# The head norm of the attention: mean squares on every row from one product with a block matrix

## The chip, the cores and the metric

One core of one Trainium2 chip runs the whole program. The metric is the device time in microseconds of one execution, from the first to the last instruction. The core has five engines that run side by side, each with a queue of its own: TensorE (PE in the profile; PEld is its loading of weights), VectorE (DVE), ScalarE (ACT), GpSimd (POOL) and SyncE (SP), which here issues the transfers. The kernel's products land in PSUM, in which it keeps eight tiles of 128 rows by 512 fp32 columns: four for the large products (`d`), three for everything else (`z`), one for the attention's sums (`acc`).

## The reference

One layer of a decoder with two head groups side by side, for a prompt of 2048 rows and for 8 x 8 sampled rows, with D = 1024:

```python
h = rmsnorm(x, norm_mix) * (1 + sc_m) + sh_m
proj = h @ w_in                                  # retention q,k,v,gate | stick-breaking q,k,v
ro = retention(...)                              # 4 heads of 128
so = sb_attention(qs, k_all, v_all, sb_bias, q_pos0)   # 8 heads of 64
so = so * lax.rsqrt(jnp.mean(so * so, axis=-1, keepdims=True) + EPS) \
    * sb_gn.reshape(H_SB, D_SB)[None, :, None, :]
mix = jnp.concatenate([ro, so], axis=-1) @ w_out
x = x + g_m * mix
# then adaLN, a gated MLP (D_FF 2816, causal convolution of width 3), residual, final RMSNorm
```

The change is in the line with `lax.rsqrt`: every head of the stick-breaking attention, 64 numbers for each token, is divided by the root of its mean square (plus EPS = 1e-6) and multiplied by a gain for each of its 64 features.

## The kernel before

All values are fp32. The large products split both operands into a high part of type fp32r and the rest, and take three of the four products (`mm3`, L295 to L297). A weight tile goes through `w_split` (L266): ACT casts the high part (`split`, L174), DVE subtracts to get the low part (`tt`, L159), both into `whl` tiles, of which there are six, two for each weight tile. Almost all tensor-tensor operations of DVE and POOL have line L159, almost all casts L174, so that they are told apart by their tiles.

The prompt is worked on in four blocks of 512 tokens. The work is written as generators, and `_weave` traces several of them side by side, each at a rate that lets all end together; the tile framework then sets the waits, and the order that each engine gets is the one that the timelines show. There are these stages:

- the start (modulation, the first rows), then the input projection `in_block` beside the attention of the sampled rows, `decode`, up to some 870 us;
- the rest of the input projection, the retention (`retention`, L966 to L1024, with `group_norm`, L939) and the attention of block 0, up to some 1260 us;
- output projection and MLP of blocks 0 to 2 (`out_block`, `ffn_block`), beside the attention of blocks 1 to 3, up to some 2935 us;
- the MLP of block 3.

`attention` goes through units (block, pair of heads j, head a of the pair, block of keys s) in four steps each. A step turns the attention weights of five steps ago (`turn`, L1150, with the split into `ahl`), multiplies those of six steps ago by the values into `acc` (`av`, L1162), and computes the scores of this one (`qk`, L1121): two sigmoids on ACT (L1124, L1125, tiles `aom` and `abe`), on POOL a mask for blocks on the diagonal (L1128, L1132) or a copy of one column (`acy`, L1135, L1141), on DVE a running product (L1138) and a multiplication (L159, `abe`). When both heads of a pair are done, `o2` holds 128 rows, two heads of 64 features, by 512 tokens, and `post` normalises it with `sb_norm` (L431 to L462), one part of it in each of the following steps of the attention: it is a generator, and its `yield` hands over to the step.

`sb_norm` before: ACT squares (L436); for each 128 tokens PE multiplies the squares by a matrix of two columns, `bo2`, which gives tokens on rows and the two heads as columns (L440, 8 columns); DVE copies them out (L442); POOL takes mean, EPS and the power -1/2 (`rstd_of`, L377 and L159 with `nhalf`, a constant tile of -0.5) and splits the result into a high and a low part (L448 to L450); PE turns it back (L454); ACT copies it (L456); PE spreads it over 128 rows with `sel4` (L459); DVE multiplies o, the gain and this (L461). In `decode` the same runs four times on 64 columns, one after the other.

Of the kernel before, what the change touches and what calls it, by code (L numbers as in the profile page):

```python
# [13 lines left out]
P = 128  # L14
# [25 lines left out]
def _consts():  # L40
# [45 lines left out]
    selb[:HS] = np.arange(HS)[:, None] == rh[None, :]  # L86
    bo2 = np.zeros((P, 2))
    bo2[:64, 0] = 1
    bo2[64:, 1] = 1
    sel4 = np.zeros((P, P))  # L90
    sel4[0, :64] = sel4[2, :64] = 1
    sel4[1, 64:] = sel4[3, 64:] = 1
    fold = np.zeros((P, 9))
# [5 lines left out]
    for t in range(NS):  # L99
        sels[1 + t // DS, t] = sels[10 + t // DS, t] = sels[18, t] = 1  # L100
    parts = dict(
        ident=ident, selb=selb, bo2=bo2, sel4=sel4, fold=fold, selp=selp, sels=sels,
        hm8=hm8, m8=m8, gsum=gsum, kdec=kdec, kdecs=kdecs, qdec=qdec, qdecs=qdecs, rowmask=rowmask,
# [16 lines left out]
class _Stream:  # L120
    """Traced work in steps; each step yields its share of the whole, or None while it has to wait."""

# [15 lines left out]
def _weave(streams, until=None):  # L138
    """Traces the streams side by side, each at the rate that lets all of them end together."""
    while any(s.live for s in streams) and (until is None or until.live):  # L140
        for s in sorted((s for s in streams if s.live), key=lambda s: s.got / s.total):
            if s.step():
                break
        else:
            raise RuntimeError("streams wait for each other")


def body(tc, I, O):
# [12 lines left out]
    def f(ap):  # L161
        return ap.bitcast(F32)
# [99 lines left out]
    def pz():  # L262
        return T(psz, [P, 512], F32, "z")

    # ------------------------------------------------------------ weights
    def w_split(src, a, b, eng=dve):  # L266
# [32 lines left out]
    def tok_mm(ps, x, w, start, stop):  # L299
        """Rows of tokens x (hi, lo) times w; a short tile has hi and lo side by side, their rows to be added."""  # L300
        if isinstance(x, tuple):
            mm3(ps, x, w, start, stop)
        else:
            pe.matmul(ps, x, w[0], start=start, stop=False)  # L304
            pe.matmul(ps, x, w[1], start=False, stop=stop)  # L305
# [40 lines left out]
    def by_tile(tiles, k0, n):  # L346
        """The products of two rows of weights with the tiles; those of the last two tile after tile."""
        order = [(k, tile) for k in range(k0, k0 + 2) for tile in tiles]
        return sorted(order, key=lambda kt: kt[1]) if k0 == n - 2 else order

    def dense_pair(wts, acts, t, features=False):
        """Two tiles of outputs, the first half of the tokens (or features) of both before the second."""
        outs = [fm_banks(t) for _ in wts]
        for h in range(2):
            for wt, out in zip(wts, outs):
                if features:
                    for ps, c0, c1 in out:
                        fm_chunk(wt, acts, ps[:, : c1 - c0], c0, c1, range(h * 4, h * 4 + 4))
                elif t == 512:
                    fm_chunk(wt, acts, out[0][0][:, h * 256 : h * 256 + 256], h * 256, h * 256 + 256)  # L360
                else:
                    ps, c0, c1 = out[h]
                    fm_chunk(wt, acts, ps[:, : c1 - c0], c0, c1)
        return outs
# [7 lines left out]

    # ------------------------------------------------------------ norms
    def rstd_of(ss, n, scale, p=P):
# [21 lines left out]
    def half_features(x, o, n, kh, A, B, acts, hpool):  # L396
        """Half kh of the columns of normalised rows, scaled and shifted, into columns o.. as hi and lo."""
        ks = slice(kh * 4, kh * 4 + 4)
# [32 lines left out]
    def sb_norm(o, n, pl, gain, tag):  # L431
        """o: [P, n], two heads of 64 rows; returns o / rms of its head * gain. Yields between its steps."""
        w = min(P, n)
        nt = n // w
        sq = T(pl, [P, n], F32, "sbsq")
        act.activation(sq, o, AF.Square)  # L436
        yield
        pm = pz()
        for t in range(nt):
            pe.matmul(pm[:w, 2 * t : 2 * t + 2], sq[:, t * w : (t + 1) * w], cc("bo2"), start=True, stop=True)  # L440
        ms = T(small, [P, 8], F32, "sbms")
        dve.tensor_copy(ms[:w, : 2 * nt], pm[:w, : 2 * nt])  # L442
        r = rstd_of(ms[:w, : 2 * nt], 2 * nt, 1.0 / DH, w)
        r4 = T(small, [P, 4, 4], F32, "sbr4")
        rh = T(small, [P, 8], F32R, "sbrh")
        rv = r[:w, : 2 * nt].rearrange("p (t a) -> p t a", a=2)
        rhv = rh[:w, : 2 * nt].rearrange("p (t a) -> p t a", a=2)
        pool.tensor_copy(rhv, rv)  # L448
        pool.tensor_copy(r4[:w, :nt, 0:2], f(rhv))
        tt(pool, r4[:w, :nt, 2:4], rv, f(rhv), ALU.subtract)  # L450
        yield
        pt = pz()
        for t in range(nt):
            pe.transpose(pt[:4, t * w : (t + 1) * w], r4[:w, t, :], ident[:w, :w])  # L454
        rt = T(pl, [P, n], F32R, "sbsq")[:4]
        act.copy(rt, pt[:4, :n])  # L456
        yield
        pb = pz()
        pe.matmul(pb[:, :n], sel4, rt, start=True, stop=True)  # L459
        out = T(pl, [P, n], F32, tag)  # L460
        dve.scalar_tensor_tensor(out, o, gain, pb[:, :n], ALU.mult, ALU.mult)  # L461
        return out  # L462

    # ------------------------------------------------------------ preparation
    def prep(pl, kp):
# [100 lines left out]

    # ------------------------------------------------------------ input projection
    def raw_features(hp, xT):
        """The first block's rows, normalised and transposed before the modulation is known."""
        for i, o, n in TILES + [(NT, TB, NS)]:  # L570
            x = T(hp, [P, D], F32, "hx")
            ld(x[:n], xp[o : o + n, :] if i < NT else xs)
            junk = T(hp, [P, D], F32, "hj")
            r = row_rstd(x, [junk[:, :512], junk[:, 512:]], n)
            dve.tensor_scalar(x[:n], x[:n], r[:n, 0:1], None, ALU.mult)
            for kh in range(2):
                ps = pz()
                for k in range(4):
                    pe.transpose(
                        ps[:, k * n : (k + 1) * n], x[:n, (kh * 4 + k) * P : (kh * 4 + k + 1) * P], ident[:n, :n]  # L580
                    )
                src = ps[:, : 4 * n].rearrange("p (k t) -> p k t", k=4)
                (act.copy if kh else dve.tensor_copy)(xT[:, kh * 4 : kh * 4 + 4, o : o + n], src)
            yield
# [165 lines left out]

    # ------------------------------------------------------------ decode attention
    def decode(dp):
# [184 lines left out]

    # ------------------------------------------------------------ retention
    def group_norm(ps, gg, qd, pl, n):  # L939
        """ps: [n, 512], four heads, each lacking its rows' decay qd; returns the gated norm of the whole."""  # L940
        mv = T(pl, [P, HR, 2], F32, "mv")
# [155 lines left out]

    # ------------------------------------------------------------ prompt attention
    def attention(blocks, tp):
# [102 lines left out]

    # ------------------------------------------------------------ output projection and MLP
    def out_block(g, xpools, fp, samp):
        """Output projection, residual and the MLP's normalised input; xpools() gives the pool of x2."""
        t = TB + (NS if samp else 0)
# [61 lines left out]
    def ffn_block(g, x2, fp, samp, after=None):  # L1268
        """The MLP and the final norm; `after` runs between the halves of the last down projection."""
        t = TB + (NS if samp else 0)  # L1270
# [123 lines left out]
    def conv_state(fi, fp):  # L1394
        """The last rows of two tiles of gates, as rows."""
        s = T(fp, [P, 512], F32, "hf")
# [22 lines left out]

    # ------------------------------------------------------------ the parts in their order  # L1420
    tile_pool = lambda name, bufs=1: tc.tile_pool(name=name, bufs=bufs, reuse_waits="tile")
    with tile_pool("in1", 2) as ip0:
        ip = _Bufs(ip0, dict(xt=2, rot=1, hf=3, st=2, kf=2, vst=1, ar=1, s18=1, gnm=1))
        with tile_pool("head", 2) as hp0:
# [17 lines left out]
            dve.tensor_scalar(nb, bb, -1.0, None, ALU.mult)  # L1442
            sel4 = T(cp, [4, P], F32R, "sel4")
            dve.tensor_copy(sel4, cc("sel4", 4))
            gnm.append(T(ip, [P, 512], F32, "gnm"))
# [61 lines left out]
class _Bufs:  # L1507
    """A pool whose tags have their own numbers of slots."""

# [9 lines left out]
class _Two:  # L1519
    """Two pools, the first for the tags given."""  # L1520

# [44 lines left out]
```

## Time and profile before

| | |
|---|---|
| median of 3 runs | 3483.96 us (3482.68 to 3484.57) |
| span of the profiled execution | 3483.6 us, 49595 instructions |
| the profiled execution's own time | given as its span alone; nothing is listed around it |
| PE, DVE, ACT, POOL busy | 3298.8, 2287.1, 1777.9, 1021.5 us |
| mean granted clock of PE | 0.979 |
| transfers | 527.72 MB, 151 GB/s over the span |

A row of a timeline has the start in us, the duration in us, engine, line, operation, output<-inputs and the count of instructions merged into it, and in brackets how long the engine sat idle before it and what ended that. A row of a stage has the stage's length, then busy time and count for PE, PEld, DVE, ACT and POOL, then the granted clock of PE, the busy share of the DMA engines, and GB/s. A row of a group has count, busy us, mean ns of one, and the idle time before them. A row of the waits has the total in us, the number of times and the longest.

### The profile page before, as it was taken

The page shows a single profiled execution, that of the slowest core. Times are in us where ns is not written, and L with a number is a line of the kernel's source. Part 1 is how long each engine was busy: PE and PEld are TensorE (multiplying, and loading weights), DVE is VectorE, ACT ScalarE, POOL GpSimd, SP SyncE. Part 2 cuts the span into 40 slices and gives each one's busy share as a digit, 9 for nine tenths or more (in the row PEclk, how much of TensorE's full clock was granted, in tenths as well). Part 3 has the DMA queues.
Part 4 walks back from the last instruction along what each step waited for, and adds up shares of the span by engine and source line. Part 5 has one row for each costly group of instructions (what it writes and reads, how often), then busy time and mean ns, then how long its engine had stood idle before and what let it go on. Part 6 is the DMA issues. An engine that isn't in the chain of part 4 may idle for free. (4 is left out here: it accounts for less than half of the span.)

```text
span 3483.6 us, 49595 instructions
## 1 busy us (share of the span) xinstructions
PE 3298.8 (95%) x17111; PEld 2693.4 (77%) x17111; DVE 2287.1 (66%) x3258; ACT 1777.9 (51%) x3153; POOL 1021.5 (29%) x1898
## 2 busy tenths in 40 slices
PE   7999999899999989999998999998899999899998
PEld 5887877776777768777877778777677777799997
DVE  5466666665665567777768777776877775545445
ACT  5457666554544456455556555554655553433323
POOL 3012011101433243434344333333433323221113
PEclk8999999999999989999999999999999999999999
DMA  6666776666756763443453333335333334332221
GB/s 226 229 198 193 234 230 218 221 223 211 210 178 194 246 196 103 121 121 112 121 182 118 118 118 112 106 112 181 109 118 106 112 103 136 112 107 88 83 86 65
DMA packets 406233, 527.72 MB, mean 151 GB/s; under 512 B 27830, under 2 KB 244009, under 8 KB 405982
## 3 DMA queue, kind: packets, MB, share of 16 engines
q1 hardware_dynamic: 405982, 524.55, 47.8%
q8 instruction: 136, 2.23, 0.3%
q14 instruction: 115, 0.94, 0.1%
HBM read 442.47 MB, written 81.99 MB: 151 GB/s over the span
## 5 line engine op out<-in xcount | busy, mean ns | idle before, releaser
L159 DVE TENSOR_TENSOR whl<-raw,whl 128x1024 fp32r<-128x1024 f32 x456 | 572.7, 1260 | 566.8 <-ACT whl L174 556.5
L174 ACT CAST whl<-raw 128x1024 fp32r<-128x1024 f32 x456 | 477.3, 1050 | 909.2 <-PE d L296 639.0
L295 PE MATMUL d<-act,whl 128*128 128x512 f32 (+2 forms) x2016 | 741.9, 369 | 5.5 <-ACT act L424 4.7
L297 PE MATMUL d<-act,whl 128*128 128x512 f32 (+2 forms) x2016 | 737.9, 366 | 4.6 <-DVE whl L159 4.6
L296 PE MATMUL d<-act,whl 128*128 128x512 f32 (+2 forms) x2016 | 735.7, 365 | 4.2 <-POOL act L159 2.2
L295 PEld LDWEIGHTS d<-act,whl 128*128 128x128 f32 x2016 | 385.8, 192 | 66.0 <-ACT act L424 6.7
L297 PEld LDWEIGHTS d<-act,whl 128*128 128x128 f32 x2016 | 385.4, 191 | 65.0 <-DVE whl L159 5.9
L296 PEld LDWEIGHTS d<-act,whl 128*128 128x128 f32 x2016 | 387.2, 192 | 60.9 <-POOL act L159 2.6
L295 PE MATMUL d<-whl,ff 128*128 128x512 f32 x704 | 280.9, 399 | 0.0
L296 PE MATMUL d<-whl,ff 128*128 128x512 f32 x704 | 280.0, 398 | 0.0
L297 PE MATMUL d<-whl,ff 128*128 128x512 f32 x704 | 279.9, 398 | 0.0
L295 PE MATMUL d<-whl,act 128*128 128x512 f32 x640 | 258.4, 407 | 14.0 <-DVE hf L159 10.8
L296 PE MATMUL d<-whl,act 128*128 128x512 f32 x640 | 259.0, 405 | 0.1
L297 PE MATMUL d<-whl,act 128*128 128x512 f32 x640 | 257.3, 403 | 0.0
L1138 DVE TENSOR_TENSOR_SCAN aom<-aom,acy 128x512 f32<-128x512 f32 x192 | 250.9, 1307 | 5.1 <-ACT aom L1124 4.6
L159 DVE TENSOR_TENSOR abe<-abe,aom 128x512 f32<-128x512 f32 (+2 forms) x320 | 234.3, 732 | 25.9 <-POOL abe L1128 5.1
L1162 PE MATMUL acc<-ahl,avv 128*128 128x512 f32 (+3 forms) x640 | 226.0, 413 | 17.6 <-ACT ahl L174 11.4
L1124 ACT ACTIVATE aom<-z,nb 128x512 f32<-128x512 f32 (+2 forms) x320 | 201.0, 628 | 73.4 <-PE z L1121 57.2
L1121 PE MATMUL z<-akk,aq 128*128 128x512 f32 (+3 forms) x640 | 193.4, 378 | 12.0 <-DVE scd L159 5.8
L1125 ACT ACTIVATE abe<-z,bb 128x512 f32<-128x512 f32 (+2 forms) x320 | 199.7, 624 | 0.0
L159 DVE TENSOR_TENSOR ahl<-z,ahl 128x512 fp32r<-128x512 f32 (+1 forms) x320 | 191.0, 597 | 11.4 <-ACT ahl L174 11.1
L159 POOL TENSOR_TENSOR ff<-ff,hf 128x512 f32<-128x512 f32 (+1 forms) x101 | 160.5, 1611 | 107.8 <-DVE hf L159 107.7
(289 smaller groups left out, 6219.4 us busy)
## 6 DMA issues: line engine op xcount, KB each, us to landing
raw<-in_w_in SPq DMA_DIRECT2D x56, 1024.0 KB
raw<-in_w_up_gate SPq DMA_DIRECT2D x44, 1024.0 KB
raw<-in_w_up_val SPq DMA_DIRECT2D x44, 1024.0 KB
akk<-k SPq DMA_DIRECT2D x160, 256.0 KB
page<-in_cache_k_pages SPq DMA_DIRECT2D x128, 256.0 KB
page<-in_cache_v_pages SPq DMA_DIRECT2D x128, 256.0 KB
raw<-in_w_down SPq DMA_DIRECT2D x32, 1024.0 KB
raw<-in_w_ada SPq DMA_DIRECT2D x24, 1024.0 KB
```

What stands on the lines that cost most here:

```text
L159: eng.tensor_tensor(o, a, b, op)
L174: act.copy(hi, src)
L295: pe.matmul(ps, sh, mh, start=start, stop=False)
L296: pe.matmul(ps, sh, ml, start=False, stop=False)
L297: pe.matmul(ps, sl, mh, start=False, stop=stop)
L1121: pe.matmul(z[:, :n], qs[g, h][:, i * P : (i + 1) * P], kk[:, c, :n], start=c == 0, stop=c == 1)
L1124: act.activation(om[:, :n], z[:, :n], AF.Sigmoid, bias=nb[:, h : h + 1], scale=-SCALE)
L1125: act.activation(be[:, :n], z[:, :n], AF.Sigmoid, bias=bb[:, h : h + 1], scale=SCALE)
L1138: dve.tensor_tensor_scan(rv, rv, rv, init, ALU.mult, ALU.bypass)
L1162: pe.matmul(accs[0][:, cs], kv[u][1][:, kt, :], m[:, cs], start=(s == g and kt == 0 and c == 0), stop=(s == 0 and kt == NT - 1 and c == 1),)
```

## The change

The mean squares of both heads come out of one product: `bo` is a 128x128 matrix with 1/64 in two blocks of 64x64 on its diagonal, so that `bo` times the squares puts the mean square of a head on each of its 64 rows, for all 512 tokens. DVE adds EPS on the way out of PSUM; POOL takes the power -1/2 of all 128x512 values in place; DVE multiplies o, the gain and the result, also in place. One tile `m` holds squares, mean squares and result one after the other. The column sums, the turn, the split and the spreading go, and with them `bo2` and `sel4`. There is an empty step between the power and the last multiplication. Both operands of the new product are plain fp32.

```diff
-    bo2 = np.zeros((P, 2))
-    bo2[:64, 0] = 1
-    bo2[64:, 1] = 1
-    sel4 = np.zeros((P, P))
-    sel4[0, :64] = sel4[2, :64] = 1
-    sel4[1, 64:] = sel4[3, 64:] = 1
+    bo = np.kron(np.eye(2), np.ones((DH, DH))) / DH
...
     def sb_norm(o, n, pl, gain, tag):
-        w = min(P, n)
-        nt = n // w
-        sq = T(pl, [P, n], F32, "sbsq")
-        act.activation(sq, o, AF.Square)
-        yield
-        pm = pz()
-        for t in range(nt):
-            pe.matmul(pm[:w, 2 * t : 2 * t + 2], sq[:, t * w : (t + 1) * w], cc("bo2"), start=True, stop=True)
-        ms = T(small, [P, 8], F32, "sbms")
-        dve.tensor_copy(ms[:w, : 2 * nt], pm[:w, : 2 * nt])
-        r = rstd_of(ms[:w, : 2 * nt], 2 * nt, 1.0 / DH, w)
-        r4 = T(small, [P, 4, 4], F32, "sbr4")
-        rh = T(small, [P, 8], F32R, "sbrh")
-        rv = r[:w, : 2 * nt].rearrange("p (t a) -> p t a", a=2)
-        rhv = rh[:w, : 2 * nt].rearrange("p (t a) -> p t a", a=2)
-        pool.tensor_copy(rhv, rv)
-        pool.tensor_copy(r4[:w, :nt, 0:2], f(rhv))
-        tt(pool, r4[:w, :nt, 2:4], rv, f(rhv), ALU.subtract)
-        yield
-        pt = pz()
-        for t in range(nt):
-            pe.transpose(pt[:4, t * w : (t + 1) * w], r4[:w, t, :], ident[:w, :w])
-        rt = T(pl, [P, n], F32R, "sbsq")[:4]
-        act.copy(rt, pt[:4, :n])
+        m = T(pl, [P, n], F32, tag)
+        act.activation(m, o, AF.Square)
         yield
         pb = pz()
-        pe.matmul(pb[:, :n], sel4, rt, start=True, stop=True)
-        out = T(pl, [P, n], F32, tag)
-        dve.scalar_tensor_tensor(out, o, gain, pb[:, :n], ALU.mult, ALU.mult)
-        return out
+        pe.matmul(pb[:, :n], cc("bo"), m, start=True, stop=True)
+        dve.tensor_scalar(m, pb[:, :n], EPS, None, ALU.add)
+        tt(pool, m, m, nhalf[:, 0:1].to_broadcast([P, n]), ALU.pow)
+        yield
+        yield
+        dve.scalar_tensor_tensor(m, o, gain, m, ALU.mult, ALU.mult)
+        return m
...
-            sel4 = T(cp, [4, P], F32R, "sel4")
-            dve.tensor_copy(sel4, cc("sel4", 4))
```

More of the change, by code (lines that the diff above doesn't have):

```diff
@@ L101, in _consts @@
     parts = dict(
-        ident=ident, selb=selb, bo2=bo2, sel4=sel4, fold=fold, selp=selp, sels=sels,
+        ident=ident, selb=selb, bo=bo, fold=fold, selp=selp, sels=sels,
         hm8=hm8, m8=m8, gsum=gsum, kdec=kdec, kdecs=kdecs, qdec=qdec, qdecs=qdecs, rowmask=rowmask,
```

## The prediction

> **What bounds the kernel now.** I read the page's first part, then the stages, then the order of time on each engine around one head norm.
>
> ```profile
> PE 3298.8 (95%) x17111; PEld 2693.4 (77%) x17111; DVE 2287.1 (66%) x3258; ACT 1777.9 (51%) x3153; POOL 1021.5 (29%) x1898
> ```
> ```profile
> 2500.00:2935.00 435.00, 430.87 (x1991) 344.89 (x1992) 327.00 (x394) 228.01 (x366) 147.31 (x249) 0.99 0.35 106
> ```
> ```profile
> 1562.13 0.39 PE L295 MATMUL d<-whl,ff 128*128 128x512 f32 x1
> ...
> 1567.49 0.40 PE L297 MATMUL d<-whl,ff 128*128 128x512 f32 x1
> ```
> ```profile
> ACT whl L174 <- PE d L296: 639.0, 226, 5.7
> ```
> TensorE (PE) is the bound: in 2500 to 2935 it is busy 430.87 of 435 us. The two matmuls are the first and last of the 24 of one split weight tile: (1567.49 - 1562.13) / 23 = 0.233 us apart, 5.6 us a tile. The wait says that ScalarE (ACT) waits for PE to give back a weight buffer (639 us in all): ACT and VectorE (DVE) run ahead of PE, by the six `whl` buffers at most. POOL, GpSimd, is 71% idle. So 1 us of PE idleness adds about 1 us to the span, and POOL costs nothing until something on PE's way waits for it.
>
> **One head norm now**, from four engines' timelines and the tile `sbsq`:
>
> ```profile
> L436 ACT ACTIVATE sbsq<-o x16: 622/632/643, 997.5 to 2913.9; 128x512 f32<-128x512 f32 x16
> ```
> ```profile
> 1540.39 0.62 ACT L436 ACTIVATE sbsq<-o 128x512 f32<-128x512 f32 x1
> ...
> 1548.01 0.56 ACT L456 CAST sbsq<-z 4x512 fp32r<-4x512 f32 x1
> ```
> ```profile
> 1541.07 1.05 PE L440 MATMUL z<-con,sbsq 128*128 128x2 f32 x8
> ...
> 1546.61 0.60 PE L454 MATMUL z<-con,sbr 128*4 128x128 f32 x4
> ...
> 1553.24 0.49 PE L459 MATMUL z<-sbsq,sel 4*128 4x512 f32 x1
> ```
> ```profile
> 1543.17 0.14 DVE L442 COPY sbms<-z 128x8 f32<-128x8 f32 x1
> ...
> 1549.28 0.67 DVE L159 TENSOR_TENSOR hf<-d,gp 128x512 f32<-128x512 f32 x1
> ...
> 1556.71 0.49 DVE L1138 TENSOR_TENSOR_SCAN aom<-aom 128x128 f32<-128x128 f32 x1 [1.25 <-POOL aom L1128]
> 1557.12 0.71 DVE L461 SCALAR_TENSOR_TENSOR sbsq<-o,vecs,z 128x512 f32<-128x512 f32 x1
> ...
> 1559.88 0.68 DVE L159 TENSOR_TENSOR ahl<-z,ahl 128x512 fp32r<-128x512 f32 x1
> ```
> ```profile
> 1544.21 1.64 POOL L159 TENSOR_TENSOR rs_b<-rs_a,nhalf 128x8 f32<-128x8 f32 x1
> ...
> 1550.02 6.38 POOL L159 TENSOR_TENSOR ff<-ff,hf 128x512 f32<-128x512 f32 x4 [3.46 <-DVE hf L159]
> ...
> 1556.39 0.29 POOL L1128 TENSOR_SCALAR_AFFINE_SELECT aom<-aom 128x128 f32<-128x128 f32 x1
> ```
> There are sixteen such norms of 128x512, one for each block and pair of heads, and four of 128x64 in the decode. The `rs_b` row is the root: a power of -1/2 on eight columns, 1.64 us. Between the square (1540.39) and the last product (1557.12) lie some 17 us in which PE mostly goes on with other tiles.
>
> **The change, part by part.** *Removed, each time:* PE's L440 (1.05 us), L454 (0.60) and L459 (0.49), DVE's copy (0.14), ACT's cast (0.56), and POOL's chain on eight columns. *Added:* one product of the 128x128 block matrix with all 512 columns, in plain fp32; a DVE add of EPS out of PSUM over 128x512; and the power over 128x512 on POOL. DVE's final L461 stays, now reading SBUF. The counts of steps agree: square, product, (empty), final.
>
> The product and the waits that go:
>
> ```profile
> L1090 PE MATMUL z<-scd,skm 64*128 64x512 f32 x16 | 7.9, 615 | 0.1
> L454 PE MATMUL z<-con,sbr 128*4 128x128 f32 x64 | 10.8, 298 | 19.1 <-POOL sbr L159 16.9 <-ACT on L956 2.2
> ```
> L1090, called 8 times, is also plain fp32 over 512 columns and shows 16 records, so two passes a call: 2 x 0.615 = 1.23 us. Against 1.05 + 0.60 + 0.49 = 2.14 that saves 0.9 us of PE, 16 x 0.9 = 14 us, and PE's idle 19.1 us in front of L454 goes: 33 us in all. The DVE add is like the 0.67 us of `hf<-d,gp`, which also reads 512 columns of PSUM; less the 0.14 us copy it adds 0.5 us to an engine that is 34% idle. I cost it at nothing beyond starting POOL later. The ACT cast's 0.56 us go from an engine that is half idle: nothing. The constant table changes by two columns, and `sel4` goes: nothing.
>
> The power is what matters. No row has it over 512 columns; these have the same instruction with the same constant over one and four columns, undisturbed, and a POOL multiplication over 512:
>
> ```profile
> 873.78 0.56 POOL L159 TENSOR_TENSOR rs_b<-rs_a,nhalf 128x1 f32<-128x1 f32 x1
> ```
> ```profile
> 1029.57 1.03 POOL L159 TENSOR_TENSOR rs_b<-rs_a,nhalf 128x4 f32<-128x4 f32 x1
> ```
> ```profile
> L159 POOL TENSOR_TENSOR c<-c,a 128x512 f32<-128x512 f32 x66 | 99.0, 1499 | 98.0 <-ACT a L1301 98.0
> ```
> One, four and eight columns take 0.56, 1.03 and 1.64 us: 0.157 us a column from one to four, 0.153 from four to eight. That is a straight line. Over 512 columns it gives 0.56 + 511 x 0.154 = 79 us. The lower bound is the multiplication, 1.5 us. I take 79: it is the same operation, and its eight columns already cost more than 512 columns of multiplying. Sixteen of these are 1270 us, and POOL has 2460 us idle, so POOL does not become the bound as a sum; it does by its order, because everything behind the power in its queue waits 79 us.
>
> Who waits? In the norm shown, the power would start at 1543.17 + 0.67, say 1543.9, and end at 1623. Behind it on POOL stand the four `ff` adds and the select of the next attention step. The scan of DVE at 1556.71 waits for that select, and L461 at 1557.12 for the power itself, so DVE, working in order, stops there. Behind them on DVE is the `ahl` of 1559.88, which PE needs here:
>
> ```profile
> 1561.24 0.71 PE L1162 MATMUL acc<-ahl,avv 128*128 128x512 f32 x2
> ```
> So PE's cover is 1561.2 - 1543.9 = 17 us. After the power come 6.38 + 0.29 us of POOL, then DVE from 1556.71 to 1560.56, 3.9 us: PE goes on at about 1634, **73 us lost**. A norm of the last block:
>
> ```profile
> 2744.96 0.14 DVE L442 COPY sbms<-z 128x8 f32<-128x8 f32 x1
> ...
> 2758.28 0.73 DVE L461 SCALAR_TENSOR_TENSOR sbsq<-o,vecs,z 128x512 f32<-128x512 f32 x1
> ...
> 2764.21 0.68 DVE L159 TENSOR_TENSOR ahl<-z,ahl 128x512 fp32r<-128x512 f32 x1
> ```
> ```profile
> 2768.81 0.71 PE L1162 MATMUL acc<-ahl,avv 128*128 128x512 f32 x2
> ```
> Power from 2745.7 to 2825; DVE stops at L461; PE at 2768.8, a cover of 23 us; DVE's list from 2758.28 to 2764.89 then takes 6.6 us, PE goes on at 2831.5: **63 us lost**. And the first block, beside the retention:
>
> ```profile
> 1005.86 0.13 DVE L442 COPY sbms<-z 128x8 f32<-128x8 f32 x1
> ```
> ```profile
> 1009.45 0.20 POOL L159 TENSOR_TENSOR va<-mv,con 128x4 f32<-128x4 f32 x1 [0.38 <-DVE mv L945]
> ```
> ```profile
> 1012.23 1.50 ACT L956 ACTIVATE on<-z,nm,rs_b 128x128 f32<-128x128 f32 x4 [4.90 <-POOL nm L953]
> ```
> ```profile
> 1013.87 0.60 PE L454 MATMUL z<-con,sbr 128*4 128x128 f32 x4 [1.24 <-ACT on L956]
> ```
> Power from 1006.6 to 1085.6. The retention's own norm (from `va`) stands behind it, ACT stops at L956 because it lacks `nm`, and PE stops at about 1013.9 because L956 holds the PSUM buffer: here PE already waits for it today. From `va` to the end of L956 are 4.3 us, so PE goes on at 1090: **76 us lost**. Four norms lie in that stage. Sum: 4 x 76 + 12 x (73 + 63) / 2 = 304 + 816 = 1120 us.
>
> PE also restarts slowly after idling. Clock is the third column from the end:
>
> ```profile
> 52.00:56.00 4.00, 4.00 (x12) 1.62 (x11) 3.08 (x4) 1.04 (x1) 3.24 (x3) 0.56 0.13 48
> 56.00:60.00 4.00, 3.60 (x32) 3.15 (x30) 2.12 (x4) 2.93 (x4) 1.82 (x3) 1.00 0.00 0
> ```
> After the idle start, one busy stretch of 4 us was granted 0.56, the next full speed: about 2 us lost a restart, 16 x 2 = 32 us. The Trainium skill ("TensorE: Matmul & The Clock Gate", Part 1) has the clock halve after an idle window and return after about 3.4 us of work, which would make this term 16 x 1.7 = 27 us by estimate, and the sum 5 us less.
>
> The four small norms of the decode follow one another:
>
> ```profile
> 852.62 0.28 DVE L461 SCALAR_TENSOR_TENSOR dm<-oT,vecs,z 128x64 f32<-128x64 f32 x1 [2.40 <-PE z L459]
> ...
> 865.92 0.28 DVE L461 SCALAR_TENSOR_TENSOR dm<-oT,vecs,z 128x64 f32<-128x64 f32 x1 [2.23 <-PE z L459]
> ```
> They come every (865.92 - 852.62) / 3 = 4.4 us. A power over 64 columns takes 0.56 + 63 x 0.154 = 10.3 us by the same line, and with square, product and the rest some 13 a norm: 4 x 8.6 = 34 us more, of which two weight tiles in hand (2 x 5.6) cover 11: 23 us.
>
> **Sum**, against the profiled span of 3483.6 us (the median of the runs, 3483.96, is the same within 0.02%): 3483.6 + 1120 + 32 + 23 - 33 = **4625.6 us**, a third slower.
>
> **Rivals.**
> *The wide power is cheap.* If POOL's cost a column fell with length, down to the multiplication's 1.5 us, the power would end long before L461 and only the savings stay: 3484 - 33 = 3451 us, faster by 0.9%. For it: only that no wide power was seen. Against it: the straight line over 1, 4 and 8. It decides below the cover of 17 us, so at 0.03 us a column, a fifth of the slope. The Trainium skill ("GPSIMD Engine Reference", section 3.1, Elementwise) gives about 2.6 cycles an element at 1.2 GHz for two-input elementwise work; by estimate 512 columns would be 1.1 us, and 3451 us the result. The multiplication's row bears that out, the eight-column power contradicts it for this operation.
>
> *PE keeps working longer.* The order of the queues can come out otherwise, with up to three weight tiles ready (six buffers, two each): 3 x 5.6 = 17 us beyond the 23 us, a cover of 40. Then 79 - 40 + 7 = 46 us a norm, 16 x 46 = 736, and 4242 us. Against it: the tiles also need DVE for PSUM and POOL for the gates.
>
> *No cover at all.* If PE stops as soon as the power starts and DVE's backlog (some 10 us, as in the first norm) comes after it: 16 x 89 = 1424, and 4930 us. For it: the first block's cover is only 7 us.
>
> **How the numbers follow.** Forecast 0.76 (own range 4400 to 4800), longer cover 0.10, no cover 0.06, cheap power 0.06, and 0.02 for a power of about the cover's length, which would end within 0.2% of before (about what a measurement of this kernel can tell from no change). Faster 0.06, same 0.02, slower 0.92. The range goes down to 4320, into the second rival, and up to 4830, towards the third.
>
> **What would show it.** A POOL row of 128x512 with the constant `nhalf`, sixteen times, near 79 us each, and a 128x64 near 10; POOL near 2270 us busy; sixteen stretches in which PE is all but idle for 60 to 76 us, behind DVE waiting for POOL; a lower granted clock right after each. L440, L454 and L459 gone, one plain fp32 product of about 1.2 us instead. I am wrong if the wide power is far from 79 us, or if PE's busy share stays near 95% while POOL is stuck.

## The result, and the profile after

The changed kernel takes 4757.57 us (median of 4 runs, 4753.89 to 4763.62) against 3484.27 us before: 1.3659 times as long, 95% interval 1.364 to 1.3679. The profiled execution's span is 4761.9 us, 1278.3 us more than the 3483.6 us before. The forecast was 4626 us, with a range of 4320 to 4830 us.

The first part of the page of the changed kernel, and from its second part the busy tenths in 40 slices for PE, POOL and PE's granted clock:

```profile
PE 3326.5 (70%) x16927; PEld 2706.4 (57%) x16927; DVE 2294.0 (48%) x3257; ACT 1769.8 (37%) x3133; POOL 2335.5 (49%) x1818
...
PE   8999999774344557337566483939385866759998
...
POOL 2110110556876565775665748473836455553112
PEclk9999999897677788678788786969697888979999
```
PE, DVE and ACT do what they did before, within 28 us. POOL does 1314 us more. Where the slices of POOL are full, those of PE and of its clock are low: PE's share of the span falls from 95 to 70%, and no other engine comes near 100%. The time is waiting, not work.

The groups of the power (line, engine, operation, tiles, shape, count, busy us, mean ns, idle time before), then some of the longest waits, in the order of their totals:

```profile
L154 POOL TENSOR_TENSOR sbsq<-sbsq,nhalf 128x512 f32<-128x512 f32 x16 | 1315.6, 82227 | 15.1 <-DVE sbsq L433 15.1
...
L154 POOL TENSOR_TENSOR dm<-dm,nhalf 128x64 f32<-128x64 f32 x4 | 42.1, 10528 | 23.3 <-DVE dm L433 23.3
```
```profile
DVE sbsq L437 <- POOL sbsq L154: 1213.2, 15, 82.6
...
ACT ff L169 <- DVE c L154: 575.8, 21, 82.9
...
PE acc L1138 <- DVE ahl L154: 400.8, 20, 79.2
...
PE z L1126 <- DVE abe L154: 296.7, 7, 74.7
```
This is the whole chain. The power lasts 82.2 us; DVE stands at the last multiplication (now L437) for fifteen of the sixteen (in the other one it stands there for 81.8 us too, but the profile puts that wait down to the POOL instruction right behind the power); ACT and PE then wait for things that DVE has behind it: the product of gate and value (`c`), the low parts of the attention weights (`ahl`), the attention weights (`abe`). One of the sixteen in order of time on POOL, DVE, ACT and PE:

```profile
2673.82 82.85 POOL L154 TENSOR_TENSOR sbsq<-sbsq,nhalf 128x512 f32<-128x512 f32 x1 [0.64 <-DVE sbsq L433]
2756.64 0.18 POOL L1111 COPY aom<-acy 128x1 f32<-128x1 f32 x1
```
```profile
2673.06 0.68 DVE L433 TENSOR_SCALAR sbsq<-z 128x512 f32<-128x512 f32 x1
2673.66 1.22 DVE L154 TENSOR_TENSOR whl<-raw,whl 128x1024 fp32r<-128x1024 f32 x1
...
2756.71 0.75 DVE L437 SCALAR_TENSOR_TENSOR sbsq<-o,vecs,sbsq 128x512 f32<-128x512 f32 x1 [81.83 <-POOL sbsq L154]
...
2759.72 0.42 DVE L154 TENSOR_TENSOR ahl<-z,ahl 128x256 fp32r<-128x256 f32 x1
```
```profile
2758.10 0.62 ACT L169 CAST ff<-c 128x512 fp32r<-128x512 f32 x1 [81.04 <-DVE c L154]
```
```profile
2682.44 0.36 PE L1138 MATMUL acc<-ahl,avv 128*128 128x256 f32 x1
2760.18 0.58 PE L1138 MATMUL acc<-ahl,avv 128*128 128x256 f32 x1 [77.38 <-DVE ahl L154]
```
On DVE one instruction stands between the addition (L433) and L437, although the program hands over to the attention's steps (`yield`) twice between them. So DVE stops at 2674.9, 1 us after the power starts. PE works on until 2682.8, a cover of 9 us, with the tile it had begun, and resumes 3.5 us after the power's end. Counting every stretch over 25 us in which PE runs no product, there are sixteen, one for each power, 70.1 to 81.3 us long, 1235 us together.

The same place as stages (length, then busy time and count for PE, PEld, DVE, ACT and POOL, then granted clock, DMA share, GB/s):

```profile
2673.00:2683.00 10.00, 9.80 (x45) 7.79 (x43) 1.88 (x3) 1.32 (x2) 9.36 (x2) 1.00 0.55 159
2683.00:2760.00 77.00, 0.00 (x0) 0.00 (x0) 3.29 (x5) 1.90 (x4) 73.81 (x2) 0.51 0.00 0
2760.00:2764.00 4.00, 3.81 (x13) 2.89 (x14) 3.90 (x6) 3.82 (x7) 1.83 (x3) 0.59 0.01 2
2764.00:2768.00 4.00, 4.00 (x20) 3.29 (x19) 4.00 (x5) 2.28 (x4) 2.01 (x2) 1.00 0.90 270
```
PE runs nothing for 77 us, the transfers stand still too, and the first 4 us afterwards are granted 0.59 of the clock. The Trainium skill ("TensorE: Matmul & The Clock Gate", Part 1) has the clock halve after an idle window and come back after some 3.4 us of work; these rows agree with it. Other restarts take longer, above all where PE still lacks work. This is the longest:

```profile
3965.00:3969.00 4.00, 2.02 (x5) 1.11 (x5) 4.00 (x7) 2.57 (x5) 1.62 (x2) 0.50 0.30 51
3969.00:3973.00 4.00, 3.40 (x8) 2.72 (x9) 3.80 (x5) 0.42 (x1) 3.37 (x3) 0.50 1.01 355
3973.00:3977.00 4.00, 4.00 (x14) 3.16 (x14) 3.90 (x4) 0.00 (x0) 4.00 (x3) 0.75 0.19 57
```
PE resumes at 3965.3, and full speed is back at about 3975.

### The profile page after: what moved, and what is told of

Its sections match the earlier page's. It is cut to its first block, busy times and chain, and to the rows that moved or that the text cites. A ratio compares the mean times of both kernels' runs of the same rounds, so it can differ in the third digit from the quotient of the medians.

```text
span 4761.9 us, 49111 instructions
## 1 busy us (share of the span) xinstructions
PE 3326.5 (70%) x16927; PEld 2706.4 (57%) x16927; DVE 2294.0 (48%) x3257; ACT 1769.8 (37%) x3133; POOL 2335.5 (49%) x1818
## 5 line engine op out<-in xcount | busy, mean ns | idle before, releaser
L154 POOL TENSOR_TENSOR sbsq<-sbsq,nhalf 128x512 f32<-128x512 f32 x16 | 1315.6, 82227 | 15.1 <-DVE sbsq L433 15.1
L437 DVE SCALAR_TENSOR_TENSOR sbsq<-o,vecs,sbsq 128x512 f32<-128x512 f32 x16 | 13.1, 821 | 1295.0 <-POOL sbsq L154 1213.2
L1126 PE MATMUL z<-con,abe 128*128 128x128 f32 x1088 | 176.6, 276 | 301.1 <-DVE abe L154 296.7
L1138 PEld LDWEIGHTS acc<-ahl,avv 128*128 128x128 f32 x640 | 107.4, 195 | 443.1 <-DVE ahl L154 412.3
L1126 PEld LDWEIGHTS z<-con,abe 128*128 128x128 f32 x1088 | 137.7, 142 | 344.0 <-DVE abe L154 299.2
L1097 PE MATMUL z<-akk,aq 128*128 128x512 f32 (+3 forms) x640 | 197.4, 384 | 169.8 <-ACT abe L1101 81.3
L290 PE MATMUL d<-whl,act 128*128 128x512 f32 x640 | 264.4, 416 | 12.6 <-DVE hf L154 12.4
L169 ACT CAST ff<-c 128x512 fp32r<-128x512 f32 (+1 forms) x88 | 55.6, 632 | 575.8 <-DVE c L154 575.8
L291 PE MATMUL d<-whl,act 128*128 128x512 f32 x640 | 263.3, 411 | 0.1
L292 PE MATMUL d<-whl,act 128*128 128x512 f32 x640 | 261.8, 409 | 0.0
```

Of the source, the lines that this page charges most:

```text
L154: eng.tensor_tensor(o, a, b, op)
L169: act.copy(hi, src)
L290: pe.matmul(ps, sh, mh, start=start, stop=False)
L291: pe.matmul(ps, sh, ml, start=False, stop=False)
L292: pe.matmul(ps, sl, mh, start=False, stop=stop)
L437: dve.scalar_tensor_tensor(m, o, gain, m, ALU.mult, ALU.mult)
```

## Experiments

Theory A: the loss is the length of one uninterrupted instruction in POOL's queue, less the work that PE has in hand, sixteen times. Its rivals: only the place of the last multiplication costs (B); something else in the change costs (C); the changes of table that a root on ACT needs would cost as well (D).

**The power replaced by a multiplication.** In the changed kernel:

```diff
-        tt(pool, m, m, nhalf[:, 0:1].to_broadcast([P, n]), ALU.pow)
+        tt(pool, m, m, nhalf[:, 0:1].to_broadcast([P, n]), ALU.mult)
```


> The changed kernel with POOL's power replaced by a multiplication with the same constant over the same columns (the root is left out). Theory A, that the whole loss is the length of the wide power in POOL's queue: 3451 us (3440 to 3465), that is 33 us faster than the kernel before, with the POOL row near 1.5 us. Rival C, that the fp32 product, the DVE pass over 512 columns or the later start of the last multiplication cost something too: above 3484 us.

Measured: 3446.08 us, 0.9894 of the kernel before (0.9874 to 0.9913). Nothing else in the change is slow: without the power it is 1% faster than before. Rival C falls.

**No root at all.** The line with the power is dropped and nothing put in its place.

> The changed kernel without the power and with nothing in its place (the root is left out): POOL has no part in the norm at all. Theory A: what the multiplication on POOL still cost is its 1.4 us a norm as a wait, so 3425 to 3440 us, between the run with the multiplication (3446) and the one with the root on ACT (3425). Rival: POOL's part is hidden, 3446 us, and the lead of the root on ACT comes from the DVE addition that it drops.

Measured: 3445.75 us, 0.9905 (0.9882 to 0.9929). The interval overlaps with that of the run with the multiplication: no cost of a POOL instruction of 1.4 us in this place is shown, so here my own expectation failed and the rival held.

**Half the columns.**

```diff
-        tt(pool, m, m, nhalf[:, 0:1].to_broadcast([P, n]), ALU.pow)
+        h = n // 2
+        tt(pool, m[:, :h], m[:, :h], nhalf[:, 0:1].to_broadcast([P, h]), ALU.pow)
```


> The changed kernel with the power taken over the first half of the columns alone (the other half keeps the mean square). Theory A: the power lasts 41 us (5.3 us in the decode) and each of the sixteen stops of PE shrinks by the same 41 us, from 77 to 36: 4757 - 16 x 41 - 4 x 5 = 4080 us. Rival: the power has a fixed large cost a call, or PE's stop isn't one for one with it: 4300 us or more.

Measured: 4090.02 us, a single run, against 4080 expected. The power's group:

```profile
L154 POOL TENSOR_TENSOR sbsq<-sbsq,nhalf 128x256 f32<-128x256 f32 x16 | 662.8, 41426 | 15.7 <-DVE sbsq L433 15.7
```
(82.227 - 41.426) / 256 = 0.159 us a column: the line that began at one, four and eight columns goes on to 512. The sixteen stops of PE last 584 us in all instead of 1235, 40.7 us less each, for 40.8 us less of power: one for one.

**The last multiplication held back.** It was queued on DVE behind the attention weights (`abe`) of a step 10 to 12 steps later, in blocks 1 to 3; `m` got a buffer of its own, `o2` two, and `abe` and `ahl` one fewer each. The edit is shortened: in block 0 and the decode the multiplication stays where it was.

```diff
         yield
-        yield
-        dve.scalar_tensor_tensor(m, o, gain, m, ALU.mult, ALU.mult)
+        for _ in range(late):                      # 10 in block 1, 12 in blocks 2 and 3
+            yield
+        with tc.issue_after(last["dve"].ins):      # the step's multiplication into abe
+            dve.scalar_tensor_tensor(m, o, gain, m, ALU.mult, ALU.mult)
```


> The changed kernel with the last multiplication of blocks 1 to 3 held back in DVE's queue, 10 to 12 attention steps behind the power (two more buffers for it, two fewer elsewhere in the attention). Theory A, that whatever stands behind the power on POOL stops PE anyway: the twelve stops shrink only from 77 us to some 65 to 72 us, 4610 to 4700 us. Rival B, that PE stops because the last multiplication itself stands at the head of DVE's queue: these twelve stops go, about 3830 us.

Measured: 4683.64 us, a single run. Its longest waits:

```profile
DVE abe L155 <- POOL aom L1117: 585.2, 8, 75.3
...
ACT aom L1106 <- POOL acy L1123: 496.1, 9, 72.7
...
DVE sbsq L443 <- POOL sbsq L155: 322.5, 4, 82.6
```
DVE no longer waits for the power itself except in block 0 (the four of the last row). In its place it and ACT wait for the one-column copies of `aom` and `acy`, which stand behind the power on POOL. PE's cover in the twelve stops grows from 8.7 to 15.9 us on the mean, and the stops shrink from 76.0 to 69.3 us. Rival B falls: what stands behind the power on POOL stops PE in any case; holding the last multiplication back, with the buffers that it needed, is worth some 7 us a norm. How much of that is the buffers' was not separated.

**The power cut up.** Sixteen pieces of 32 columns in blocks 1 to 3, one for each attention step, each queued behind that step's own small POOL instruction, and the last multiplication behind the last piece; buffers as in the run before. The edit is shortened: block 0 and the decode keep one piece.

```diff
-        tt(pool, m, m, nhalf[:, 0:1].to_broadcast([P, n]), ALU.pow)
-        yield
+        for i in range(16):
+            p = m[:, i * 32 : (i + 1) * 32]
+            with tc.issue_after(last["pool"].ins):  # for all but the first piece
+                tt(pool, p, p, nhalf[:, 0:1].to_broadcast([P, 32]), ALU.pow)
+            yield
```


> The changed kernel with the power of blocks 1 to 3 cut into sixteen pieces of 32 columns, one for each attention step, each queued on POOL behind that step's own small POOL instruction, and the last multiplication behind the last piece (buffers as in the run with the late multiplication). POOL does the same sum of work, some 5.5 us a piece by the slope of 0.159 us a column. Theory A, that the length of one uninterrupted block decides and not POOL's sum: the twelve stops of 61 to 75 us go; pieces and POOL's other 2 to 3 us a step are a little more than a step of 7 us, which may cost up to 16 x 12 x 1.5 = 290 us: 3830 to 4120 us. Rival C, that POOL's sum of time or the wide power as such costs: 4600 us or more.

Measured: 4260.62 us, a single run, above the range of theory A and far below that of its rival. The pieces, and a stretch of 200 us of block 2's attention:

```profile
L155 POOL TENSOR_TENSOR sbm<-sbm,nhalf x192: 5406/5416/6419, 1726.6 to 3700.9; 128x32 f32<-128x32 f32 x192
```
```profile
2500.00:2700.00 200.00, 172.19 (x743) 135.56 (x744) 126.18 (x158) 88.70 (x147) 171.41 (x130) 0.91 0.30 90
```
POOL's sum is that of the changed kernel (2351.2 us on the page against 2335.5), and eleven of the twelve long stops are gone; none over 14 us is left in their place. But these stops were worth some 11 x 76 = 836 us, and the time falls by only 497 us against the changed kernel, so a good part of the loss comes back in another form. POOL is now busy 86% of this stretch, and PE 86%. In this stretch DVE waits for POOL's masks (`aom`), and PE for `ahl`, which comes through the same queue of DVE:

```profile
DVE aom L1126 <- POOL aom L1116: 31.8, 8, 9.4
...
PE acc L1150 <- DVE ahl L155: 22.2, 6, 11.3
```
So the unbroken length makes the long stops, but a POOL that is nearly full costs too; how the rest divides among such short waits was not measured. The twelfth long stop shows the theory once more. The last norm comes when the attention has no steps left behind which pieces could be queued, so its pieces stand in a row:

```profile
3620.19 86.11 POOL L155 TENSOR_TENSOR sbm<-sbm,nhalf 128x32 f32<-128x32 f32 x16 [3.65 <-DVE sbm L434]
```
With these 86 us of pieces in one block PE stops for 74 us, as it does in the changed kernel.

**The decode alone.** The kernel before, with the new norm in `decode` and the old one in the attention (the selecting matrix is loaded by itself).

> The kernel before with the new norm in the decode alone, four norms of 64 columns; the attention keeps the old one. Theory A: each of the four takes some 13 us instead of 4.4 and PE has work for about 11 us of the 36: 3505 to 3515 us. Rival: the decode's norms are hidden beside the input projection: 3484 us.

Measured: 3506.01 us, 1.0073 (1.0056 to 1.009), 24 us over the 3481.57 us of before beside it.

**The root kept narrow, spread by the turn.** In the kernel before, shortened at the `...` by the tiles that go and the size of one:

```diff
...
-        pool.tensor_copy(rhv, rv)
-        pool.tensor_copy(r4[:w, :nt, 0:2], f(rhv))
-        tt(pool, r4[:w, :nt, 2:4], rv, f(rhv), ALU.subtract)
-        yield
-        pt = pz()
-        for t in range(nt):
-            pe.transpose(pt[:4, t * w : (t + 1) * w], r4[:w, t, :], ident[:w, :w])
-        rt = T(pl, [P, n], F32R, "sbsq")[:4]
-        act.copy(rt, pt[:4, :n])
+        rb = T(pl, [P, nt * 2 * DH], F32, "sbsq")
+        pool.tensor_copy(
+            rb[:w].rearrange("p (a d) -> p a d", d=DH), r[:w, : 2 * nt].unsqueeze(2).to_broadcast([w, 2 * nt, DH])
+        )
         yield
         pb = pz()
-        pe.matmul(pb[:, :n], sel4, rt, start=True, stop=True)
+        for t in range(nt):
+            pe.transpose(pb[:, t * w : (t + 1) * w], rb[:w, t * P : (t + 1) * P], ident[:w, :w])
+        yield
```


> The kernel before with one part of the change's aim and the narrow root kept: the eight roots are copied out to 64 columns each on POOL (one copy of 128x512, about 1 us, instead of cast, copy and subtraction), and PE's turn of that puts them on their rows at once; no product with the selecting matrix, no ACT cast. Theory A: 16 x 0.25 to 0.5 us of PE and a few us of waits go, 3470 to 3482 us against 3484. Rival: POOL's copy starts PE's turn later, and PE waits in front of it as long as before or longer: 3484 to 3495 us.

Measured: 3459.38 us, 0.9947 (0.993 to 0.9963): faster than before by more than expected. Where the rest of the gain comes from is open.

**The root on ACT.** In the changed kernel; `epsb` is a constant tile of EPS.

```diff
-        dve.tensor_scalar(m, pb[:, :n], EPS, None, ALU.add)
-        tt(pool, m, m, nhalf[:, 0:1].to_broadcast([P, n]), ALU.pow)
+        act.activation(m, pb[:, :n], AF.Abs_reciprocal_sqrt, bias=epsb[:, 0:1])
```


> The changed kernel with the root taken by ACT out of PSUM (the reciprocal root function with EPS as bias, 128x512) instead of DVE's addition and POOL's power. Theory A: it costs ACT some 0.65 us and two changes of function table a norm, on an engine that is idle half the time, so it comes near the run with the multiplication: 3446 to 3470 us. Rival D, that the changes of table stop ACT ahead of the attention's sigmoids and PE pays for them: 16 x 2 x 1.3 = 42 us more, about 3488 us.

Measured: 3425.28 us, 0.9838 (0.9826 to 0.9851), faster than both kernels, than the kernel without a root (0.9905, on another chip, each against the kernel before beside it) and than expected. The root, and the changes of function table by the line that needed one:

```profile
L435 ACT ACTIVATE sbsq<-z,epsb x16: 687/689/690, 987.5 to 2859.0; 128x512 f32<-128x512 f32 x16
```
```profile
L435 ACT ACT_TABLE_LOAD x17 | 21.8, 1283 | 0.9 <-PE z L434 0.6
L1101 ACT ACT_TABLE_LOAD x13 | 16.7, 1283 | 0.2
```
Two further runs were to say why. In one ACT only adds EPS (`AF.Identity`, no other table); the other repeats the root on ACT beside it.

> The kernel with the root on ACT, but ACT only adds EPS on the way out of PSUM, by a function that needs no other table (the root is left out). It separates the root's tables from the move from DVE to ACT. If the 23 us between no root with DVE's addition (0.9905 of before) and the root on ACT (0.9838) come from taking DVE's pass away: at most 0.984 of before, and less by what the table changes cost, which is up to 42 us if they stop PE: 3385 to 3428 us. If they come from another order of the queues alone: 3435 to 3450 us.

Measured: 3428.04 us, 0.985 (0.9833 to 0.9866).

> The kernel with the root on ACT once more, beside the run with ACT's addition on the same chip. Expected 0.9838 of before, within 0.003 of it. Rival: its lead over the shorter variant (0.9867) was the chip's, then nearer 0.987 to 0.990.

Measured: 3428.48 us, 0.9854 (0.9838 to 0.9871). With and without the root ACT takes the same time, so the table changes, 1.283 us each, are hidden, and rival D falls. The lead over the kernel without a root (0.9905) goes with the move of the pass from DVE to ACT; whether it is DVE's 0.67 us or the new order of the queues that brings it was not separated.

**One `yield` fewer**, on top of the root on ACT (its expectation calls both `yield`s empty steps):

> The kernel with the root on ACT, with one of the two empty steps taken out ahead of the last multiplication. Theory A (the queues' order is not that of the steps, so an empty step is no cover): no difference from the run with two, 3420 to 3430 us. Rival: DVE meets the last multiplication earlier and waits for ACT's root: 3430 to 3445 us.

Measured: 3432.81 us, 0.9867 (0.9844 to 0.989). The time lies in the range of the rival, but the interval overlaps those of the two runs with both `yield`s; no difference is shown.

## Why the prediction was right, and by how much its terms were off

The mechanism was the one forecast: the power's line over 1, 4 and 8 columns, POOL's queue, DVE in order behind it, PE idle sixteen times. By its steps:

| term | forecast | measured |
|---|---|---|
| the power over 512 columns | 79 us | 82.2 us |
| over 64 columns | 10.3 us | 10.5 us |
| PE's cover, block 0 | 7 us | 6.0 us |
| PE's cover, blocks 1 to 3 | 17 and 23 us | 8.7 us (mean) |
| from the power's end to PE, block 0 | 4.3 us | 4.6 us |
| from the power's end to PE, blocks 1 to 3 | 10.6 and 6.6 us | 2.5 us (mean) |
| the sixteen stops together | 1120 us | 1235 us |
| decode | 23 us | 24 us (alone) |
| the sixteen restarts together | 32 us | some 50 us (estimate, below) |
| saved beside the power | 33 us | 33 to 37 us (by the ratios of the two runs without a root) |

*The term that was off most* is the cover in blocks 1 to 3: 20 us on the mean in the forecast, 8.7 measured, which makes 12 x 11.3 = 136 us too little. I took the order of DVE's queue from the kernel before, where the last multiplication stands 13 us behind the start of the root and DVE clears several other things first. In the changed kernel the same steps of the program give another order, with none to three other instructions between L433 and L437 in those blocks (one in the norm shown).

In block 0 the sizes held. In two of its four stops PE waits at the end as forecast, for the line of ACT that lacked `nm` (now L932), and in the other two for DVE (`S` and `rmh`). One of the first two:

```profile
1132.25 2.07 PE L968 MATMUL z<-qT,kT 128*128 128x128 f32 x8 [80.68 <-ACT on L932]
```
*The way back* in blocks 1 to 3 was sized too long, 8.6 us on the mean against 2.5, and that takes 12 x 6.1 = 73 us back again. In the norm shown only the copy of one column (0.18 us) follows the power on POOL, where I had put 6.38 + 0.29 us. *The power* itself was 3.2 us short, 16 x 3.2 = 51 us, because the slope of the first columns (0.154 us) is a little under that of the long ones (0.159). Together that is the 115 us by which the sixteen stops were short. That the two readings of the old order err in opposite directions is luck: with the way back alone put right, the forecast would have been 73 us further off.

The run that held the multiplication back has stops of 69.3 us, near the 68 us that the forecast had used, but this does not confirm the working: its power lasts 82.3 us, its cover is 15.9 and its way back 3.0 us, against 79, 20 and 8.6.

*The restarts* were put at 2 us each, 32 us. The span's 1278 us less the stops' 1235 us, less 24 us of the decode and plus 33 us of savings, leave 52 us. Over the first 12 us behind each of the sixteen stops the granted clock is 0.60 to 0.88, short of full speed by 1.4 to 4.8 us a restart and by 44 us in all, and PE is idle for another 15 us there. So slow restarts account for about all of what is left, and the 2 us had been read off a single restart.

*The rivals.* The cheap power is refuted by its row; its price of 3451 us was the time of the kernel without a root (3446), so the savings were sized rightly in total. Their two parts were not measured apart. The rule that it could have come from, the Trainium skill's ("GPSIMD Engine Reference", section 3.1) 2.6 cycles an element, comes near the multiplication (1.1 us by estimate, 1.3 to 1.5 us measured) and not this operation: by estimate, 0.159 us a column at the page's 1.2 GHz would be 191 cycles. The longer cover did not come by itself. No cover at all was nearer than I gave it credit for: DVE had 1 us in the norm shown, PE 3 to 14 us.

## What to carry to other kernels

Price an instruction by the same operation at two or three sizes, not by another operation at the right size: the multiplication over 512 columns said 1.5 us, the power over 1, 4 and 8 said 79, and it took 82. A long instruction on an idle engine isn't free: what counts is its unbroken length against the work that the bound engine has in hand, and that is read from the queues of the new kernel, because steps between two lines of a program need not become distance in a queue. Cutting the instruction up helps only as far as its engine has room beside the pieces: here 497 us came back of some 836. When a wide transcendental is wanted, look which engine has it as one pass: ACT did the 512 columns in 0.69 us, with two changes of table a norm that the time did not show.

## What the runs showed of the hardware

- POOL's power costs 0.159 us a column of 128 rows, in a straight line: 5.4 us at 32, 10.5 at 64, 41.4 at 256 and 82.2 at 512 columns.
- The 30 changes of ACT's function table shown for the root on ACT, 1.283 us each and 38.5 us in all, moved the time by nothing that could be measured (0.985 without, 0.9838 and 0.9854 with).
- In the 77 us in which PE was idle the granted clock was 0.51; it was 0.59 in the next 4 us and 1.00 after that. Over the first 12 us behind the sixteen such stops it was 0.60 to 0.88.
